# A two-layer encoder on one core: large tiles moved to multiples of 128 bytes, and a 64-row product given all 128 rows

## The chip, the core and the metric

The kernel runs on one core of a Trainium2 chip. The metric is the device time of one execution in microseconds (us), the median of several runs. Engines are named as in the profile: PE is TensorE (matmuls), PEld its weight loads, DVE is VectorE, ACT is ScalarE, SP issues most of the DMAs.

## What is computed

256 tokens of width 2048 go through two layers in float32. Each layer has a token mixer and a gated channel mixer with a short convolution:

```
x = x + rms_norm(mixer(rms_norm(x)))
x = x + rms_norm((gelu(conv3(h @ w_up_gate)) * (h @ w_up_val)) @ w_down)     h = rms_norm(x), d_ff 5632
```

The mixer of layer 0 has 8 heads of windowed attention and 8 query heads of grouped attention, head size 128. The mixer of layer 1 is latent attention with 16 heads. There a query and a key have 128 plain and 64 rotary dimensions, and the rotary key is shared by all heads:

```
q = concat(q_nope, rope(q_rope))        # 128 + 64
k = concat(k_nope, rope(k_rope))        # k_rope is the same for all heads
s = q @ k.T * 192 ** -0.5;  o = softmax(s) @ v
```

## The kernel before

**Products in parts.** Every float32 operand `a` of a matmul is split into a high part (a copy to float32r, on ACT) and a low part (`a` minus the high part, on DVE), and a product is made of three: high x high, high x low, low x high. `_split` (L117, L118) does this to each weight chunk of 128 x 1024, which SP loads into `raw`; the parts are `whi` and `wlo`, three buffers each. Four loops use them:
- `proj_tok` with `mm3` (L172 to L174): the stationary operand is a 128 x 128 piece of the activations (`xhl` before the mixers, `oh` and `ol` for the attention's output, `gh` and `gl` for the gated values), the moving one 512 columns of `whi` or `wlo`. It makes the input projections and all output projections.
- `proj_t` (L186, L187): stationary weights, moving activations. `xhl` holds high and low part side by side, so L186 streams 512 columns (both) against `whi` and L187 256 columns (high) against `wlo`. It makes the up-projections, 2816 pairs in the two layers.
- `proj_small` and `proj_pair` (L172 to L174 with 256 columns): the latent projections from `cq` and `ckv`.
- `attend` (L475 scores, L256 transposes, L172 to L174 with `pT` and `v`): one call for each of 32 heads, two half heads of 128 queries each.

**The rotary part of a score.** For a half head of layer 1 `scores` lists five products: three of the plain parts (`qk`), and two of the rotary parts. A rotary query in `qr` has its high part in rows 0 to 63 and its low part in rows 64 to 127. `kr[:, 0, :]` holds the high part of the key twice, in both halves of the rows; one 128-row matmul so makes high x high and low x high. `kr[:, 1, :]` holds the low part twice, and of it only rows 0 to 63 are wanted, with the query's high part: a 64-row matmul. `evac_kr` fills `kr` with one copy from PSUM (L819).

**Order.** Python generators hand out the attention's and the norms' steps between weight chunks (`tick`), and each engine runs its list in the order in which it was made. At the end of an output projection `out_proj` computes the norm's factor for each half of the tokens (`factor`, with its columns `posta`, `posts`, `postv`, `postu`), turns the new `x` by transposes, and fills waits of TensorE with matmuls on `zeros`.

**Where tiles lie.** Pools lie one behind the other in each partition of the on-chip memory, and a tile takes a multiple of 32 bytes. `const` holds `gains` (1664 bytes) and then `eps` and `spare` (32 bytes each); `act`, `wp` (weights) and `small` (columns, rows) follow, and the pools of a mixer or a ffn lie behind `small`. The table gives the first byte of each tile modulo 128, as built; all slices that a matmul takes begin at multiples of 128 bytes from it.

| tiles | before | after |
|---|---|---|
| `gains` | 0 | 0 |
| `zeros`, `ident`, `ident_r` | 64 | 0 |
| `xhl`, `m`, `qk`, `x`, `raw`, `whi`, `wlo` | 64 | 0 |
| in `small`: `junk`, `m3` | 0, 96 | 96, 64 |
| `gb` | 32 | 0 |
| all tiles of the mixers and ffns: `oh`, `ol`, `gh`, `gl`, `cq`, `ckv`, `kr`, `qr`, `q`, `k`, `kB`, `v`, `vB`, `p`, `pT`, `y`, tables | 96 | 0 |

Of the kernel before, what the change touches and what calls it, by code (L numbers as in the profile page):

```python
# [9 lines left out]
F32 = mybir.dt.float32  # L10
# [6 lines left out]
P = 128  # L17
# [20 lines left out]
class Model:  # L38
# [307 lines left out]
    def out_proj(self, nk, parts, post, pre, order=None, before={}):  # L346
# [6 lines left out]
        nc = self.nc  # L353
# [26 lines left out]
        r = []  # L380

        def factor(t):
            acc, s, v, u = (self.col(f"post{n}") for n in "asvu")
            r.append(self.col("postr"))
            self.square_sums(acc, ps[t])
            nc.scalar.activation(s, acc, AF.Sqrt, scale=1.0 / D, bias=part[:, t:t + 1])
            nc.vector.tensor_scalar(out=v, in0=acc, scalar1=1.0 / D, scalar2=part[:, t:t + 1],
                                    op0=ALU.mult, op1=ALU.add)
            nc.vector.scalar_tensor_tensor(out=u, in0=s, scalar=s, in1=v, op0=ALU.mult, op1=ALU.add)
            nc.vector.reciprocal(out=u, in_=u)  # L390
            return nc.vector.tensor_scalar(out=r[t], in0=s, scalar1=2.0, scalar2=u, op0=ALU.mult, op1=ALU.mult)
# [5 lines left out]

        full = slice(0, 512)
        factor(0)
        if pre is None:  # L400
            scaled(3, 0)
# [337 lines left out]
    def mixer1(self, pre):  # L739
        nc, tc, a = self.nc, self.tc, self.a  # L740
        with tc.tile_pool(name="mix1", bufs=1) as sp:
# [6 lines left out]
            cq = sp.tile([P, 4, 2, T], F32R, name="cq")  # L748
            ckv = sp.tile([P, 4, 2, T], F32R, name="ckv")
            kr = sp.tile([P, 2, T], F32R, name="kr")  # L750

            def latent(ps, row, out):
                g = sp.tile([P, 512], F32, tag="grow", name="grow", bufs=1)
                nc.sync.dma_start(out=g, in_=a["lat"][row:row + 1, :].broadcast_to([P, 512]))
                ss = self.small.tile([P, 2, 1], F32, tag="ls", name="ls", bufs=2)
                for t in range(2):
                    self.square_sums(ss[:, t, :], ps[t])
                rr = self.rstd_over(ss, self.r, 1, 512)
                whole = []
                for t in range(2):  # L760
                    y = sp.tile([P, 512], F32, tag="y", name="y", bufs=2)
                    nc.vector.scalar_tensor_tensor(out=y, in0=ps[t], scalar=rr[:, t, :], in1=g,
                                                   op0=ALU.mult, op1=ALU.mult)
                    whole.append(y)
                yield
                for k in range(0, 4, 2):
                    pt = self.psum("at").rearrange("p (i t) -> p i t", i=2)
                    for j in range(2):
                        for t in range(2):
                            self.turn_whole(pt[:, j, t * P:(t + 1) * P], whole[t][:, (k + j) * P:(k + j + 1) * P])  # L770
                    self.parted(out[:, k:k + 2, 0, :], out[:, k:k + 2, 1, :], pt)

            def rope(y, z, v, n):

                nc.vector.tensor_tensor(out=y, in0=v, in1=tab[:, :, 0].broadcast_to([P, 2, n, 64]), op=ALU.mult)
                for h in range(2):
                    d, f = slice(32 * h, 32 * h + 32), slice(32 - 32 * h, 64 - 32 * h)
                    nc.vector.tensor_tensor(out=z[:, :, :, d], in0=v[:, :, :, f],
                                            in1=tab[:, :, 1, :, d].broadcast_to([P, 2, n, 32]), op=ALU.mult)
                nc.vector.tensor_tensor(out=y, in0=y, in1=z, op=ALU.add)  # L780

            def room(tag, n):
                t = sp.tile([P, 512], F32, tag=tag, name=tag, bufs=2 if tag == "y" else 1)
                return t[:, :2 * n * 64].rearrange("p (t h f) -> p t h f", t=2, f=64)
# [12 lines left out]
            def evac_kr(ps):  # L797

                k, y, z = (room(tag, 1) for tag in ("grow", "y", "z"))
                raw = sp.tile([P, 512], F32, tag="p", name="raw", bufs=self.p_bufs)[:64]  # L800
                nc.scalar.copy(raw[:, T:], ps[:64, T:])
                nc.vector.tensor_tensor(out=raw[:, :T], in0=ps[:64, :T], in1=raw[:, T:], op=ALU.add)
                yield
                v = self.psum("at")[:, :2 * 64].rearrange("p (t f) -> p t f", t=2)
                for t in range(2):
                    nc.tensor.transpose(v[:, t, :], raw[:, t * P:(t + 1) * P], self.ident[:64, :64])
                hl = sp.tile([P, 2, 512], F32R, tag="hl", name="hl", bufs=2)
                tok = hl[:, 0, :].rearrange("p (t a b f) -> p t a b f", t=2, a=2, b=2)
                for t in range(2):
                    nc.scalar.activation(k[:, t, 0, :], v[:, t, :], AF.Copy, scale=self.r[:, t:t + 1])  # L810
                rope(y, z, k, 1)
                for b in range(2):
                    self.parted(tok[:, :, 0, b, :], tok[:, :, 1, b, :], y[:, :, 0, :])
                yield
                pt = self.psum("at", F32R).rearrange("p (a t) -> p a t", a=2)
                for b in range(2):
                    for t in range(2):
                        self.turn(pt[:, b, t * P:(t + 1) * P], tok[:, t, b].rearrange("p b f -> p (b f)"))
                nc.scalar.copy(kr, pt.bitcast(F32))  # L819

            def evac_qr(v, qr):
                v = v.rearrange("p t (h f) -> p t h f", f=64)
# [21 lines left out]
            for p in range(8):  # L844
                if p % 2 == 0:
                    qr = []
                    evqr = self.evac(evac_qr(self.proj_small(part(cq), 256, 4), qr), 1, heads[-8:-4])
                qk, v, v_gen = [], [], []

                def evac_qk(w, src, qk=qk, p=p):  # L850
                    if not qk:
                        qk.append(self.act.tile([P, 2, 2, 2, T], F32R, tag=f"xm{p % 4}", name="qk"))
                    self.parted(qk[0][:, src, :, 0, :], qk[0][:, src, :, 1, :], w)
                    yield

                def evac_v(w, v=v):
                    v.append(sp.tile([P, 2, 2, 256], F32R, tag="v", name="v", bufs=3))
                    self.parted(v[0][:, 0], v[0][:, 1], w)
                    yield

                eq = self.evac(evac_qk(self.proj_pair(part(cq)), 0), 1, heads[-8:-6])
                if p == 0:
                    self.finish(evkv)
                ek = self.evac(evac_qk(self.proj_pair(part(ckv)), 1), 1, (eq,))

                def head(h, qk=qk, v=v, qr=qr, v_gen=v_gen):
                    i = h % 2

                    def scores(b):
                        bs = slice(b * P, (b + 1) * P)  # L870
                        qt, kt = qk[0][:, 0, i], qk[0][:, 1, i]
                        return [(qt[:, 0, bs], kt[:, 0, :]), (qt[:, 0, bs], kt[:, 1, :]), (qt[:, 1, bs], kt[:, 0, :]),
                                (qr[0][:, h % 4, bs], kr[:, 0, :]), (qr[0][0:64, h % 4, bs], kr[0:64, 1, :])]

                    s = slice(i * P, (i + 1) * P)
                    yield from self.attend(scores, scale, None, lambda j: (v[0][:, 0, j, s], v[0][:, 1, j, s]),
                                           v_gen, o(h), sp)

                new = [self.later(head(h), (evkr, evqr, eq, ek)) for h in (2 * p, 2 * p + 1)]
                v_gen.append(self.evac(evac_v(self.proj_small(part(ckv), 256, 4)), 1, heads[-6:-4]))  # L880
                heads += new
# [38 lines left out]
    def run(self):  # L920
        nc, a = self.nc, self.a
        self.plan(self.all_chunks())
        self.x, self.xhl = [None] * 4, [None] * 4
        self.g = self.const.tile([P, G_ALL], F32, name="gains")
        nc.scalar.dma_start(out=self.g, in_=a["gains"])
        self.eps = self.const.tile([P, 1], F32, name="eps")
        nc.vector.memset(self.eps, EPS)
        self.spare = self.const.tile([P, 1], F32, name="spare")
        self.table(AF.Sqrt, self.eps)
        self.zeros = self.const.tile([P, T], BF16, name="zeros")  # L930
        nc.vector.memset(self.zeros, 0.0)
        self.warm(24)
        self.mixer0("l0_ffn_pre")
        self.ffn(0, "l1_mix_pre")
        self.mixer1("l1_ffn_pre")
        self.ffn(1, None)
        assert self.at == len(self.chunks)
# [81 lines left out]
```

## Time and profile before

| | |
|---|---|
| three runs | 2113.58, 2104.84, 2113.62 us; median 2113.58 |
| profiled execution | 2104.7 us, of which the span from first to last instruction 2102.9 |
| mean granted TensorE clock in it | 0.999 |
| busy: PE, DVE, ACT | 2090.2, 1342.3, 1081.8 us |
| HBM read | 381.96 MB, 183 GB/s over the span |

A busy TensorE is not a TensorE at its peak: the records of neighbouring matmuls overlap (a row of 394 ns begins 0.23 us ahead of the next), so the distance from one start to the next is the time that one takes. Rows of the order in time show start, duration, engine, line, operation, names (out, then moving and stationary operand, or the two of a tile alike), rows x columns of the stationary operand, and partitions x columns of the moving one.

### The profile page before, as it was taken

The page shows a single profiled execution, that of the slowest core. Times are in us where ns is not written, and L with a number is a line of the kernel's source. Part 1 is how long each engine was busy: PE and PEld are TensorE (multiplying, and loading weights), DVE is VectorE, ACT ScalarE, POOL GpSimd, SP SyncE. Part 2 cuts the span into 40 slices and gives each one's busy share as a digit, 9 for nine tenths or more (in the row PEclk, how much of TensorE's full clock was granted, in tenths as well). Part 3 has the DMA queues.
Part 4 walks back from the last instruction along what each step waited for, and adds up shares of the span by engine and source line. Part 5 has one row for each costly group of instructions (what it writes and reads, how often), then busy time and mean ns, then how long its engine had stood idle before and what let it go on. Part 6 is the DMA issues. An engine that isn't in the chain of part 4 may idle for free.

```text
span 2102.9 us, 29245 instructions
## 1 busy us (share of the span) xinstructions
PE 2090.2 (99%) x11121; PEld 1775.0 (84%) x11121; DVE 1342.3 (64%) x2050; ACT 1081.8 (51%) x1694; POOL 0.2 (0%) x4
## 2 busy tenths in 40 slices
PE   9999999999999999999999999999999999999998
PEld 7888888888888888888888998788888888888886
DVE  6876757667667676444476775676766667654444
ACT  7654546555555555334465554565555555544433
POOL 0000000000000000000000000000000000000000
PEclk9999999999999999999999999999999999999999
DMA  8545565666666666666665335566666666666664
GB/s 315 169 151 170 160 204 160 196 192 184 194 190 185 195 184 194 193 190 194 192 180 157 117 117 164 171 191 192 186 192 192 188 192 190 187 193 190 193 189 150
DMA packets 108718, 385.97 MB, mean 184 GB/s; under 512 B 12065, under 2 KB 12577, under 8 KB 108577
## 3 DMA queue, kind: packets, MB, share of 16 engines
q1 hardware_dynamic: 108288, 383.83, 60.4%
q8 instruction: 87, 1.43, 0.3%
q14 instruction: 55, 0.44, 0.1%
q10 hardware_dynamic: 288, 0.28, 0.0%
HBM read 381.96 MB, written 2.10 MB: 183 GB/s over the span
## 4 chain that ended last, share of the span: by engine, by line
PE 99%; DVE 1%; DMA 0%; ACT 0%; issue 0%; DVEq 0%; SPq 0%
PE ps L186 31%; PE ps L174 16%; PE ps L172 16%; PE ps L173 16%; PE ps L187 15%; PE ps L475 2%; PE ps L256 1%; DVE x L395 0%; PE ps L417 0%; DMA raw<-in_w_in 0%; PE ps L792 0%; PE ps L252 0%; ACT junk L296 0%; DVE xhl L529 0%; PE ps L793 0%
## 5 line engine op out<-in xcount | busy, mean ns | idle before, releaser
L118 DVE TENSOR_TENSOR wlo<-raw,whi 128x1024 fp32r<-128x1024 f32 (+1 forms) x710 | 867.3, 1222 | 702.0 <-ACT whi L117 700.5
L117 ACT CAST whi<-raw 128x1024 fp32r<-128x1024 f32 (+1 forms) x710 | 743.7, 1048 | 817.7 <-PE ps L174 439.4
L186 PE MATMUL ps<-xhl,whi 128*128 128x512 f32 x2816 | 978.6, 394 | 1.0 <-DVE xhl L529 1.0
L187 PE MATMUL ps<-xhl,wlo 128*128 128x256 f32 x2816 | 779.2, 277 | 0.0
L186 PEld LDWEIGHTS ps<-xhl,whi 128*128 128x128 f32 x2816 | 527.6, 188 | 123.3 <-DVE xhl L529 2.0
L187 PEld LDWEIGHTS ps<-xhl,wlo 128*128 128x128 f32 x2816 | 528.7, 188 | 1.1 <-DVE wlo L118 0.5
L174 PE MATMUL ps<-whi,gl 128*128 128x512 f32 x704 | 280.9, 399 | 0.0
L173 PE MATMUL ps<-wlo,gh 128*128 128x512 f32 x704 | 277.4, 394 | 0.0
L172 PE MATMUL ps<-whi,gh 128*128 128x512 f32 x704 | 276.0, 392 | 0.0
L173 PEld LDWEIGHTS ps<-wlo,gh 128*128 128x128 f32 x704 | 132.2, 188 | 34.2
L172 PEld LDWEIGHTS ps<-whi,gh 128*128 128x128 f32 x704 | 132.2, 188 | 31.6
L174 PEld LDWEIGHTS ps<-whi,gl 128*128 128x128 f32 x704 | 132.2, 188 | 30.4
L172 PE MATMUL ps<-whi,xhl 128*128 128x512 f32 x352 | 138.9, 396 | 1.0 <-ACT whi L117 1.0
L173 PE MATMUL ps<-wlo,xhl 128*128 128x512 f32 x352 | 137.4, 390 | 0.0
L174 PE MATMUL ps<-whi,xhl 128*128 128x512 f32 x352 | 137.4, 391 | 0.0
L172 PE MATMUL ps<-whi,oh 128*128 128x512 f32 x256 | 102.3, 400 | 0.0
L174 PE MATMUL ps<-whi,ol 128*128 128x512 f32 x256 | 100.8, 394 | 0.0
L173 PE MATMUL ps<-wlo,oh 128*128 128x512 f32 x256 | 100.5, 393 | 0.0
L261 ACT COPY half<-ps 128x256 f32<-128x256 f32 x176 | 65.0, 369 | 45.7 <-PE ps L186 36.0
L172 PEld LDWEIGHTS ps<-whi,xhl 128*128 128x128 f32 x352 | 66.0, 188 | 14.7 <-ACT whi L117 1.3
L174 PEld LDWEIGHTS ps<-whi,xhl 128*128 128x128 f32 x352 | 66.0, 188 | 14.1
L173 PEld LDWEIGHTS ps<-wlo,xhl 128*128 128x128 f32 x352 | 66.2, 188 | 13.5 <-DVE wlo L118 0.9
(183 smaller groups left out, 1642.7 us busy)
## 6 DMA issues: line engine op xcount, KB each, us to landing
raw<-in_w_up SPq DMA_DIRECT2D x352, 512.0 KB, 4.2
raw<-in_w_down SPq DMA_DIRECT2D x176, 512.0 KB, 3.7
raw<-in_w_in SPq DMA_DIRECT2D x88, 512.0 KB, 3.7
raw<-in_w_out SPq DMA_DIRECT2D x64, 512.0 KB, 3.7
gb<-in_post SPq DMA_DIRECT2D x16, 256.0 KB, 3.6
raw<-in_w_qn SPq DMA_DIRECT2D x8, 512.0 KB, 3.7
raw<-in_w_kn SPq DMA_DIRECT2D x8, 512.0 KB, 3.7
raw<-in_w_v SPq DMA_DIRECT2D x8, 512.0 KB, 3.7
```

The source lines that it names most:

```text
L117: self.nc.scalar.copy(hi[:, s], raw[:, s])
L118: self.nc.vector.tensor_tensor(out=lo[:, s], in0=raw[:, s], in1=hi[:, s].bitcast(F32), op=ALU.subtract)
L172: mm(ps, lh, rh, start=start, stop=False)
L173: mm(ps, lh, rl, start=False, stop=False)
L174: mm(ps, ll, rh, start=False, stop=stop)
L186: mm(out[i], hi[:, s], x(k), start=k == 0, stop=False)
L187: mm(out[i][:, :T], lo[:, s], x(k)[:, :T], start=False, stop=k == nk - 1)
L256: self.tc.keep_in_program_order(self.nc.tensor.transpose(out, x, self.ident))
L261: self.nc.scalar.copy(b, ps[:, T:])
L475: nc.tensor.matmul(ps[:, i, :], l, r, start=n == 0, stop=n == len(pairs) - 1))
```

## The change

It moves tiles and changes one product:
- `eps` and `spare` become two columns of one tile `one` in the pool `small`, and the four columns of `factor` become one tile `post` of four columns. `const` then holds 64 bytes less ahead of what follows, and `small` is a multiple of 128 bytes long; the table above gives what comes of it.
- The rotary high queries times low keys product takes all 128 rows. Rows 64 to 127 of `kr[:, 1, :]` are set to zero by a memset, and `evac_kr` copies to `kr` in two pieces that leave them alone.

```
         def factor(t):
-            acc, s, v, u = (self.col(f"post{n}") for n in "asvu")
+            cols = self.col("post", 4)
+            acc, s, v, u = (cols[:, n:n + 1] for n in range(4))
             r.append(self.col("postr"))
...
             kr = sp.tile([P, 2, T], F32R, name="kr")
+            nc.vector.memset(kr[64:, 1, :].bitcast(F32), 0.0)
...
-                nc.scalar.copy(kr, pt.bitcast(F32))
+                nc.scalar.copy(kr[:, 0, :], pt[:, 0, :].bitcast(F32))
+                nc.scalar.copy(kr[0:64, 1, :], pt[0:64, 1, :].bitcast(F32))
...
-                                (qr[0][:, h % 4, bs], kr[:, 0, :]), (qr[0][0:64, h % 4, bs], kr[0:64, 1, :])]
+                                (qr[0][:, h % 4, bs], kr[:, 0, :]), (qr[0][:, h % 4, bs], kr[:, 1, :])]
...
-        self.eps = self.const.tile([P, 1], F32, name="eps")
+
+        one = self.small.tile([P, 2], F32, name="one", bufs=1)
+        self.eps, self.spare = one[:, 0:1], one[:, 1:2]
         nc.vector.memset(self.eps, EPS)
-        self.spare = self.const.tile([P, 1], F32, name="spare")
         self.table(AF.Sqrt, self.eps)
```

TensorE's and SP's instructions stand in the same order as before. DVE and ACT have one more each. On DVE it stands at the end of the first ffn, between the two calls of `factor` (L388 to L392 are one call's four columns; L396 adds the half of the tokens to `x`). After the change:

```order
L396 SCALAR_TENSOR_TENSOR x_342<-m_9209,postr,x_342 128x512
L118 TENSOR_TENSOR wlo<-raw,whi 128x1024
L752 MEMSET kr 64x256
L388 TENSOR_SCALAR post<-post,part 128x1
L390 SCALAR_TENSOR_TENSOR post<-post 128x1
L391 RECIPROCAL post<-post 128x1
```

The memset is the row that is new there. On ACT the copy to `kr` stands in the latent mixer between the parts of `qk` and the next weights' high part. Before:

```order
L523 CAST hl<-y 128x2x64 x2
L523 CAST qk<-ps 128x2x256
L819 CAST kr<-ps 128x512
L117 CAST whi<-raw 128x1024
L523 CAST hl<-y 128x8x64
```

And after:

```order
L524 CAST hl<-y 128x2x64 x2
L524 CAST qk<-ps 128x2x256
L821 CAST kr<-ps 128x256
L822 CAST kr<-ps 64x256
L117 CAST whi<-raw 128x1024
L524 CAST hl<-y 128x8x64
```

One copy has become two; nothing else there moved.

## The prediction

> **What bounds the kernel now.** I read the page first: busy shares and the chain of waits. Then the table of who waited for whom, and last the order of time on TensorE, because what matters here is how far apart its matmuls start.
>
> ```profile
> PE 2090.2 (99%) x11121; PEld 1775.0 (84%) x11121; DVE 1342.3 (64%) x2050; ACT 1081.8 (51%) x1694; POOL 0.2 (0%) x4
> PE 99%; DVE 1%; DMA 0%; ACT 0%; issue 0%; DVEq 0%; SPq 0%
> PE ps L417 <- DVE x L395: 1.4, 3, 0.7
> DVE wlo L118 <- ACT whi L117: 700.5, 535, 2.4
> ACT whi L117 <- PE ps L174: 439.4, 270, 3.0
> L186 PE MATMUL ps<-xhl,whi 128*128 128x512 f32 x2816 | 978.6, 394 | 1.0 <-DVE xhl L529 1.0
> L187 PE MATMUL ps<-xhl,wlo 128*128 128x256 f32 x2816 | 779.2, 277 | 0.0
> L174 PE MATMUL ps<-whi,gl 128*128 128x512 f32 x704 | 280.9, 399 | 0.0
> L172 PE MATMUL ps<-whi,xhl 128*128 128x512 f32 x352 | 138.9, 396 | 1.0 <-ACT whi L117 1.0
> L172 PE MATMUL ps<-whi,oh 128*128 128x512 f32 x256 | 102.3, 400 | 0.0
> ```
>
> TensorE is 99% of the chain, and its longest total wait for anyone is 1.4 us. DVE waits for ACT and ACT waits for TensorE, so those two run behind it with room to spare. Whatever shortens the distance between two matmuls shortens the span one for one; whatever happens on DVE, ACT or a queue costs nothing until TensorE waits for it. In the groups the mean of one (394 ns) is no guide, since neighbours overlap: I use the distance of starts instead. A name such as `whi,gl` is moving operand, then stationary one. L172 to L174 are issued in equal numbers for each pair of operands, so the groups stand for 3 x 704, 3 x 352 and 3 x 256 matmuls.
>
> The distances, taken from the first and the last row of steady stretches on TensorE:
>
> ```profile
> 25.83 0.39 PE L172 MATMUL ps<-whi,xhl 128*128 128x512 f32 x1
> ...
> 33.99 0.39 PE L172 MATMUL ps<-whi,xhl 128*128 128x512 f32 x1
> ...
> 289.80 0.40 PE L172 MATMUL ps<-whi,oh 128*128 128x512 f32 x1
> ...
> 297.50 0.40 PE L172 MATMUL ps<-whi,oh 128*128 128x512 f32 x1
> ...
> 500.14 0.28 PE L187 MATMUL ps<-xhl,wlo 128*128 128x256 f32 x1
> ...
> 507.77 0.28 PE L187 MATMUL ps<-xhl,wlo 128*128 128x256 f32 x1
> ...
> 899.63 0.39 PE L172 MATMUL ps<-whi,gh 128*128 128x512 f32 x1
> ...
> 907.33 0.39 PE L172 MATMUL ps<-whi,gh 128*128 128x512 f32 x1
> ...
> 1072.26 1.25 PE L156 MATMUL ps<-zeros 128*128 128x256 bf16 x10
> 1073.35 0.60 PE L417 MATMUL ps<-ident,x 128*128 128x128 f32 x4
> ...
> 1151.82 0.29 PE L172 MATMUL ps<-whi,ckv 128*128 128x256 f32 x1
> ...
> 1154.35 0.28 PE L172 MATMUL ps<-whi,ckv 128*128 128x256 f32 x1
> ...
> 1247.09 0.28 PE L173 MATMUL ps<-ckv,whi 128*128 128x256 f32 x1
> ...
> 1249.55 0.28 PE L173 MATMUL ps<-ckv,whi 128*128 128x256 f32 x1
> 1249.67 0.28 PE L174 MATMUL ps<-ckv,wlo 128*128 128x256 f32 x1
> 1249.79 0.28 PE L172 MATMUL ps<-pT,v 128*128 128x256 f32 x1
> ...
> 1251.11 0.28 PE L174 MATMUL ps<-pT,v 128*128 128x256 f32 x1
> ```
>
> Beside each pair stands where its operands lie (bytes mod 128, from the table of the kernel's layout):
> - 512 columns, moving 64, stationary 64 (`whi,xhl`): 36 steps in 8.16 us, 226.7 ns each.
> - 512 columns, moving 64, stationary 96 (`whi,oh` and `whi,gh`): 33 steps in 7.70 us, 233.3 ns each, both times.
> - 256 columns, 64 and 96 (`whi,ckv`): 21 steps in 2.53 us, 120.5 ns; 96 and 96 (`pT,v`): 11 steps in 1.32 us, 120.0 ns; 96 and 64 (`ckv,whi`): 21 steps in 2.46 us, 117.1 ns.
> - up-projection, a 512 and a 256 together, all at 64: 22 pairs in 7.63 us, 346.8 ns.
> - floor: ten bf16 matmuls of 256 columns in 1.09 us, 109.0 ns; so at most 218.0 ns for 512 columns.
>
> So a stationary operand at 96 costs 6.7 ns more than one at 64 where 512 columns stream, and about 3 ns more where 256 do; the moving operand at 96 shows no cost (117.1 is the lowest of its kind). No row shows a float32r operand at 0.
>
> **The change, part by part.** *The 64-row product.* 32 matmuls take 64 rows of `qr` and `kr`:
>
> ```profile
> L475 PE MATMUL ps<-kr,qr 64*128 64x256 f32 x32 | 12.2, 382 | 0.0
> L475 PE MATMUL ps<-kr,qr 128*128 128x256 f32 x32 | 9.0, 282 | 0.0
> 1146.90 0.62 PE L475 MATMUL ps<-qk 128*128 128x256 f32 x3
> 1147.35 0.59 PE L475 MATMUL ps<-kr,qr 128*128 128x256 f32 x2
> 1147.87 0.62 PE L475 MATMUL ps<-qk 128*128 128x256 f32 x3
> ...
> 1148.85 0.63 PE L475 MATMUL ps<-qk 128*128 128x256 f32 x3
> ```
>
> From 1146.90 to 1148.85 run two half heads of five matmuls each, 0.975 us per half head. Five 256-column matmuls without the 64-row form take 5 x 120.0 = 600 ns (the `pT,v` rows), so the one 64-row matmul, with the change of form before and after it, costs 375 ns. With 128 rows all five have one form: 32 x 0.375 = 12.0 us, all of it TensorE's own time. The 100 ns between the two means (382 and 282) would give only 3.2 us; I take the larger, since the distances contain the neighbours' delay and the means do not.
>
> A rule that speaks against this part: the Trainium skill, TensorE: Matmul & The Clock Gate, section LDWEIGHTS (loading the stationary operand), says that a load's time follows the columns and not the contraction rows. By that rule alone 64 rows cost what 128 do, this part brings 0 and the sum below would be 12.0 us higher; the 0.975 us of the half head disagrees.
>
> What it adds: a memset on DVE ahead of the second `factor` of the first ffn, and a second copy on ACT.
>
> ```profile
> 1071.58 1.22 DVE L118 TENSOR_TENSOR wlo<-raw,whi 128x1024 fp32r<-128x1024 f32 x1
> 1072.75 0.21 DVE L387 TENSOR_SCALAR postv<-posta,part 128x1 f32<-128x1 f32 x1
> 1072.02 0.60 ACT L296 ACTIVATE junk<-ps 128x512 bf16<-128x512 f32 x1 [1.75 <-PE ps L174]
> 1140.40 0.59 ACT L819 CAST kr<-ps 128x512 fp32r<-128x512 f32 x1 [0.53 <-PE ps L252]
> ```
>
> The memset waits for the last matmul of the ffn, and the square sum on ACT (1072.02) waits for the same one. DVE's next instruction, at 1072.75, needs that square sum, so DVE has an instruction's room there: by the nearest row, 0.2 us (256 elements without an input), it may finish by then or come a tenth late. The split at 1071.58 ends at 1072.80, so in the worst case `factor` starts 0.2 us later and TensorE, which here spins on the ten filler matmuls, ends 0.2 us later. The copy of 0.59 us becomes two, so at most 0.6 us more of ACT; ACT stood idle 0.53 us before it, and the first heads' scores (1146.90, above) follow over 5 us later. I count 0 for both, 0.3 us at most. The four `post` columns in one tile and `one` for `eps` and `spare` add no wait: the built program waits for the same events.
>
> *The offsets.* Order and number of all other instructions stay. Stationary operands that go from 96 to 0 take, at least, the place of those at 64: (2112 + 768) x (233.3 - 226.7) = 19.2 us. The 256-column ones with a stationary at 96 are, from the code, 32 x 6 for `pT,v`, 96 scores in layer 0, 64 of `kr,qr`, 192 of `whi,ckv` and 96 of `whi,cq`: 640 x 2.9 = 1.9 us.
>
> Unknown is what 0 gives against 64. Lower end: nothing, since 64 and 0 may be the same to the reader. Upper end: all down to the floor: 2816 x (346.8 - 327.0) = 55.8; 1056 x (226.7 - 218.0) = 9.2; 2880 x (233.3 - 218.0) = 44.1; 640 x 11.0 = 7.0; the 480 with stationary 64, x 8.1 = 3.9: in all 120.0 in place of 21.1 us. A loss is bounded by the row at 96 (a rival, below). I take the lower end, because the row nearest to an operand at 0 is one at 64 with both operands alike, and one more set of rows says that part of the excess at 64 is not the address:
>
> ```profile
> 1106.35 0.39 PE L173 MATMUL ps<-wlo,xhl 128*128 128x512 f32 x1
> ...
> 1107.51 0.39 PE L172 MATMUL ps<-whi,xhl 128*128 128x512 f32 x1
> ...
> 1109.32 0.39 PE L174 MATMUL ps<-whi,xhl 128*128 128x512 f32 x1
> ```
>
> Just behind a group of transposes the same operands at 64 first run 5 steps in 1.16 us, 232 ns each, and then 8 in 1.81 us, 226 ns each. The distance there settles with how loads and streams fall against each other, and a shift of both by the same 64 bytes leaves that as it is.
>
> Sum: 12.0 + 19.2 + 1.9 = 33.1 us off the profiled execution's 2104.7 us (span 2102.9): 2071.6. Two of the three timed runs lie 8.9 us above that execution (2113.6; the median), one at it; I add half of this, 4.4, and say 2076.
>
> **The rivals.**
> 1. Offsets from 128-byte lines count in full, and 0 reaches the floor. For it: the excess over 218.0 falls with the offset, 15.3 at 96 and 8.7 at 64. Against it: the rows behind the transposes, where the excess changes and the offsets don't, and the moving operand, which at 96 costs no more than at 64. Price: 12.0 + 120.0 = 132.0 off, 1972.7. With a floor a little lower for 512 columns than twice that of 256, 1960.
> 2. Offsets do nothing; `gh` and `oh` cost 233.3 for another reason, such as their distance from `whi`. Then only the 64-row part is left: 2092.7. The same comes out of the Trainium skill, SBUF — State Buffer, section SBUF: two separate sides, which gives the memory lines of 16 bytes: every offset here, before and after, is a multiple of 16. The 6.7 ns between 64 and 96 disagree.
> 3. Slower: an operand at 0 costs what one at 96 does. The 512-column matmuls now at 64 rise to 233.3: (1056 + 2816) x 6.6 = 25.6 more, 12.0 less, the others unchanged: 2118.3. It decides from 5.8 ns on for each of the 3872 (12.0 + 10.5, half a per cent). For it: no row at 0. Against it: alike offsets (64 and 64) are the quickest 512-column rows.
> 4. The 64-row part brings nothing, because the delay belongs to five matmuls from five tiles and not to the form: 2083.6. Against it: `pT,v` and the scores of layer 0 show no such stretch.
>
> **How the numbers follow.** Chances: the forecast 0.55, rival 1 0.27, rival 2 0.10, rival 3 0.05, rival 4 0.03. The range has to take in rival 1, without which 0.27 would be left out, and reaches at the other end to rival 2 with the 8.9 us of the slower runs: 1960 to 2100. The forecast's own range is 2062 to 2086. Half a per cent, 10.5 us, is about what a measurement of this kernel tells from no change. Faster: 0.55 + 0.27 + 0.06 of rival 2 (12.0 us is near that bound) + 0.03 = 0.91; same 0.05; slower 0.04.
>
> **What would show it.** Right: `whi,gh` and `whi,oh` start 226.7 ns apart, the up-projection's pair stays at 347, a half head takes 0.60 us, and no 64-row form is left in the groups. Rival 1: the pair falls to some 327 and `whi,xhl` to 218 or less. Wrong altogether: `whi,gh` still at 233.3 (rival 2), `whi,xhl` above 227 (rival 3), or TensorE waiting over 1 us for DVE near the first ffn's end.

## The result, and the profile after

The changed kernel takes 2074.4 us, the median of four runs (2074.27 to 2074.60). The four runs of the kernel before beside it had a median of 2109.2 us (two at 2104.8, two at 2113.6), which gives a ratio of 0.9835 with an interval of 0.9806 to 0.9864. Runs of one kernel lie on levels 9 us apart, and the experiments below show which instructions make that step; so I compare the lowest levels: 2104.8 with 2074.4, 30.4 us, and the profiled spans, 2102.9 with 2072.8, 30.1 us. The forecast was 2076.

The page of the changed kernel, the lines that answer to those shown of before: busy time of TensorE and its weight loads, the share of the chain of waits, and the costliest groups (busy time, mean of one, idle time ahead).

```profile
PE 2060.3 (99%) x11121; PEld 1772.1 (85%) x11121; DVE 1341.7 (65%) x2051; ACT 1083.5 (52%) x1695; POOL 0.2 (0%) x4
PE 98%; DVE 1%; DMA 0%; issue 0%; ACT 0%; DVEq 0%; SPq 0%
L186 PE MATMUL ps<-xhl,whi 128*128 128x512 f32 x2816 | 978.6, 394 | 1.0 <-DVE xhl L530 1.0
L187 PE MATMUL ps<-xhl,wlo 128*128 128x256 f32 x2816 | 779.2, 277 | 0.0
L174 PE MATMUL ps<-whi,gl 128*128 128x512 f32 x704 | 273.9, 389 | 0.0
L172 PE MATMUL ps<-whi,xhl 128*128 128x512 f32 x352 | 138.9, 396 | 0.5 <-ACT whi L117 0.5
L172 PE MATMUL ps<-whi,oh 128*128 128x512 f32 x256 | 99.9, 390 | 0.0
```

TensorE does as many matmuls as before and is still the whole chain. Two groups moved, `whi,gl` (280.9 to 273.9) and `whi,oh` (102.3 to 99.9); the up-projection and `whi,xhl` read the same to the last digit. These are durations that overlap, so the size of the gain has to be read from starts. Four places in the order of time on TensorE: the down-projection, the up-projection, the half heads of the first latent scores, and a 256-column projection.

```profile
889.72 0.39 PE L172 MATMUL ps<-whi,gh 128*128 128x512 f32 x1
...
892.44 0.39 PE L172 MATMUL ps<-whi,gh 128*128 128x512 f32 x1
...
499.61 0.40 PE L186 MATMUL ps<-xhl,whi 128*128 128x512 f32 x1
...
506.20 0.39 PE L186 MATMUL ps<-xhl,whi 128*128 128x512 f32 x1
...
1137.88 0.52 PE L476 MATMUL ps<-qk 128*128 128x256 f32 x3
1138.24 0.40 PE L476 MATMUL ps<-kr,qr 128*128 128x256 f32 x2
1138.48 0.52 PE L476 MATMUL ps<-qk 128*128 128x256 f32 x3
...
1139.08 0.52 PE L476 MATMUL ps<-qk 128*128 128x256 f32 x3
...
1141.60 0.28 PE L172 MATMUL ps<-whi,ckv 128*128 128x256 f32 x1
...
1144.36 0.28 PE L174 MATMUL ps<-whi,ckv 128*128 128x256 f32 x1
```

`whi,gh`: 12 steps in 2.72 us, 226.7 ns (233.3 before). Up-projection: 19 pairs in 6.59 us, 346.8 ns (346.8). A half head of five matmuls: 0.60 us (0.975). `whi,ckv`: 23 steps in 2.76 us, 120.0 ns (120.5).

Adding up the distance from each matmul's start to the next one's start, over the whole trace, gives the account (my sums over all 11121 matmuls, us; the total is about 9.5 us short of the span: 1.1 us ahead of the first matmul and 8.4 us behind the start of the last):

```
group of matmuls                      before    after   change   forecast
weights x gh,gl,oh,ol  (512 columns)   672.0    653.1    -18.9      -19.2
weights x xhl          (512 columns)   243.7    243.6     -0.1        0
up-projection pairs    (512 and 256)   985.7    985.7      0          0
kr,qr and qk                            31.1     19.7    -11.4      -12.0
other 256-column matmuls               116.6    116.5     -0.1       -1.9
transposes and fillers                  44.4     44.9     +0.4        0 (0.3 at most)
sum                                                      -30.0      -33.1
```

### The profile page after: what moved, and what is told of

The parts are those of the page before. It is cut to its first block, busy times and chain, and to the rows that moved or that the text cites. A ratio compares the mean times of both kernels' runs of the same rounds, so it can differ in the third digit from the quotient of the medians.

```text
span 2072.8 us, 29247 instructions
## 1 busy us (share of the span) xinstructions
PE 2060.3 (99%) x11121; PEld 1772.1 (85%) x11121; DVE 1341.7 (65%) x2051; ACT 1083.5 (52%) x1695; POOL 0.2 (0%) x4
## 4 chain that ended last, share of the span: by engine, by line
PE 98%; DVE 1%; DMA 0%; issue 0%; ACT 0%; DVEq 0%; SPq 0%
PE ps L186 31%; PE ps L172 16%; PE ps L173 16%; PE ps L174 16%; PE ps L187 16%; PE ps L476 1%; PE ps L256 1%; DVE x L396 1%; PE ps L418 0%; DMA raw<-in_w_in 0%; PE ps L794 0%; DVE wlo L118 0%; PE ps L252 0%; ACT junk L296 0%; DVE xhl L530 0%
## 5 line engine op out<-in xcount | busy, mean ns | idle before, releaser
L172 PE MATMUL ps<-whi,gh 128*128 128x512 f32 x704 | 273.9, 389 | 0.0
L174 PE MATMUL ps<-whi,gl 128*128 128x512 f32 x704 | 273.9, 389 | 0.0
L173 PE MATMUL ps<-wlo,gh 128*128 128x512 f32 x704 | 273.9, 389 | 0.0
L172 PE MATMUL ps<-whi,oh 128*128 128x512 f32 x256 | 99.9, 390 | 0.0
```

The lines of the kernel that those rows point to most:

```text
L172: mm(ps, lh, rh, start=start, stop=False)
L173: mm(ps, lh, rl, start=False, stop=False)
L174: mm(ps, ll, rh, start=False, stop=stop)
```

## The experiments

Two theories ran through them. By theory L it is an operand's own offset from a memory line that costs time; by theory R it is the distance between the addresses of the moving and the stationary operand of one matmul, and where both lie together does not matter. The kernel before could not tell them apart: its 226.7 ns rows had both operands at 64, its 233.3 ns rows one at 64 and one at 96.

**e1, the 64-row part alone; e2 and e8, the offsets alone.** e1 is the kernel before with the memset, the two copies and the full-row product. e2 is the changed kernel with these three taken back; e8 is the same kernel run again, for a second profile.

```
e1, in the kernel before:
+            nc.vector.memset(kr[64:, 1, :].bitcast(F32), 0.0)
-                nc.scalar.copy(kr, pt.bitcast(F32))
+                nc.scalar.copy(kr[:, 0, :], pt[:, 0, :].bitcast(F32))
+                nc.scalar.copy(kr[0:64, 1, :], pt[0:64, 1, :].bitcast(F32))
-                ... (qr[0][0:64, h % 4, bs], kr[0:64, 1, :])]
+                ... (qr[0][:, h % 4, bs], kr[:, 1, :])]
```

> The kernel before with the 128-row product alone; all tiles stay at 64 and 96. Theory of the prediction (the 64-row form costs 375 ns per half head, nothing else): the profiled span falls by 11.4 to 12.0 us to some 2091, gh and oh stay at 233.3 ns. Rival (the part of the change that counts is the offsets, the rows bring the 3.2 us of the means): 2099. If the two parts help or hinder each other, this run and the next do not add up to the 30.1 us of the whole change.

> The changed kernel with the 64-row product put back; all large tiles at 0. Theory of the prediction: gh and oh at 226.7 ns, span 18.9 us less than before (some 2084), the half head of layer 1 still 0.975 us. Rival (the gain of gh and oh needs nothing but other work beside it, not the offsets): no gain, 2103.

> The kernel of the second run once more, for a profile of one of its longer executions (2095 us in three of four, 2086 in the other). If the 9 us are a steady state of the up-projection as in the run with all tiles at 96, one layer's 1390 pairs are at 353 ns and the other's at 347, with the same operands; if not, the 9 us stand elsewhere.

e1 took 2092.25 us (span 2090.4, ratio 0.9913, interval 0.9883 to 0.9942), 12.5 us of span off. e2 took 2086.39 us once and 2095.2 to 2095.4 three times (ratio 0.9917, 0.9885 to 0.9948); the profiled execution was the quick one, span 2084.6, 18.3 us off. e8 took 2095.32 us. The two parts add up: 12.5 + 18.3 = 30.8 against 30.1. From the groups of e1 and then of e2:

```profile
L475 PE MATMUL ps<-kr,qr 128*128 128x256 f32 x64 | 12.8, 281 | 0.0
L174 PE MATMUL ps<-whi,gl 128*128 128x512 f32 x704 | 280.9, 399 | 0.0
```

```profile
L174 PE MATMUL ps<-whi,gl 128*128 128x512 f32 x704 | 273.9, 389 | 0.0
```

In e1 `whi,gl` stands where it stood before, in e2 where it stands after. In e1 the distances of `kr,qr` and `qk` fell by 11.7 us, those of the other 256-column matmuls by 0.8, and no other group moved by more than 0.2. In e2 the distances of `gh`, `gl`, `oh` and `ol` fell by 18.8 us, and all others rose by 0.5.

**e3, all large tiles together at 96.** One pad of 24 elements behind the gains moves every large tile of the changed kernel by 96 bytes, so that all distances between operands stay what they were.

```
         nc.scalar.dma_start(out=self.g, in_=a["gains"])
+        self.const.tile([P, 24], F32, name="pad0")
```

> The changed kernel with 96 unused bytes ahead of all tiles: every large tile at 96, moving and stationary operands alike. Theory R (what counts is where the two operands of a matmul lie relative to each other): no change, 2074, all 512-column matmuls with xhl, gh, oh at 226.7 ns. Theory L (a stationary operand at 96 crosses one line more than one at 0 or 64): all 512-column matmuls 6.6 ns longer: 1056 + 2880 + 2816 of them, 44.6 us, 2119.

It took 2083.4 to 2083.5 us three times and 2092.4 once (ratio 0.9882, 0.985 to 0.9913). The order of time of e3 on TensorE, the down-projection first and then the up-projection of each layer:

```profile
889.64 0.39 PE L172 MATMUL ps<-whi,gh 128*128 128x512 f32 x1
...
893.04 0.39 PE L172 MATMUL ps<-whi,gh 128*128 128x512 f32 x1
...
499.89 0.39 PE L186 MATMUL ps<-xhl,whi 128*128 128x512 f32 x1
...
506.47 0.40 PE L186 MATMUL ps<-xhl,whi 128*128 128x512 f32 x1
...
1499.82 0.40 PE L186 MATMUL ps<-xhl,whi 128*128 128x512 f32 x1
...
1506.54 0.40 PE L186 MATMUL ps<-xhl,whi 128*128 128x512 f32 x1
```

With both operands at 96, `whi,gh` starts every 226.7 ns (15 steps in 3.40 us), just as at 0. Theory L falls, and theory R holds for this term. The 8.9 us that e3 took more than the changed kernel are elsewhere: 19 pairs of the up-projection take 6.58 us in layer 0 (346.3 ns) and 6.72 us in layer 1 (353.7 ns), with the same code and the same offsets. Over each layer's 1390 pairs the sums are 483.4 and 492.4 us.

**e4, e5, e6, the weights alone shifted.** A pad ahead of the weight buffers and one behind them put `raw`, `whi` and `wlo` at 64, 32 or 96 past a line. The pads also moved `gh`, `gl`, `oh` and `ol` to 128 past a multiple of 256, so that their distance is not the weights' shift alone: moving minus stationary address, modulo 256, is 192, 160 and 224 for them in e4, e5 and e6, it is 192, 224 and 160 for the pairs, and 64, 32 and 96 for weights x `xhl`.

```
+        self.wp.tile([P, s // 4], F32, name="pad0")                       # s = 64, 32, 96
+        self.small.tile([P, (128 - s) // 4], F32, name="pad1", bufs=1)
```

> The changed kernel with the weight tiles (raw, whi, wlo) at 64 and all others at 0: the operands of every weight matmul lie 64 apart, the stationary ones at 0 (xhl, gh, oh, latents) or at 64 (weights). Theory L: 64 is as good as 0, no change, 2074. Theory R with a period of 64 bytes: no change either. Theory R with a period of 128 bytes: the 512-column matmuls change; from the one row that is known, 32 apart costs 6.6 ns, so up to 6.6 ns for each of 6752, 44.6 us more, or if 64 apart is a better place than 0, up to 8.7 ns less for each.

> The changed kernel with the weight tiles at 32 and all others at 0. The moving weights of the projections lie 32 bytes above their stationary operands, the moving activations of the up-projections 32 below. Theory R (the place of the two operands relative to each other, period 128): the up-projections, 32 below like gh and oh before, take 6.7 ns more a pair in both layers, 18 us; for the projections (3936 matmuls, 32 above) no run has shown it yet: 0 if only 'below' costs, 2092; 26 us more if the distance counts and not its sign, 2118. Theory S (the steady state that a stretch falls into is chance, and offsets only shift the chance): gh and oh at 226.7 or 233.3 by chance, the two layers not alike.

> The changed kernel with the weight tiles at 96 and all others at 0, the mirror of the run before: projections with the moving operand 32 below the stationary one (as gh and oh before the change), up-projections 32 above. Theory R: gh, oh and also xhl of the input projections at 233.3 ns, 3936 x 6.6 = 26 us more; the up-projections at 347 if only 'below' costs (2100), at 353 if the distance counts (2118).

They took 2109.9 us (ten runs, ratio 1.0007, 0.9992 to 1.0022), 2118.35 (four, 1.0057, 1.0037 to 1.0078) and 2096.95 (seven, 0.9958, 0.9945 to 0.9971), each within 0.3 us from run to run. Down-projection and up-projection of e4, then of e5, then of e6:

```profile
889.76 0.39 PE L172 MATMUL ps<-whi,gh 128*128 128x512 f32 x1
...
892.56 0.39 PE L172 MATMUL ps<-whi,gh 128*128 128x512 f32 x1
...
499.84 0.40 PE L186 MATMUL ps<-xhl,whi 128*128 128x512 f32 x1
...
506.55 0.40 PE L186 MATMUL ps<-xhl,whi 128*128 128x512 f32 x1
```

```profile
889.61 0.39 PE L172 MATMUL ps<-whi,gh 128*128 128x512 f32 x1
...
893.12 0.40 PE L172 MATMUL ps<-whi,gh 128*128 128x512 f32 x1
```

```profile
499.91 0.39 PE L186 MATMUL ps<-xhl,whi 128*128 128x512 f32 x1
...
506.50 0.39 PE L186 MATMUL ps<-xhl,whi 128*128 128x512 f32 x1
...
890.13 0.40 PE L172 MATMUL ps<-whi,gh 128*128 128x512 f32 x1
...
892.93 0.40 PE L172 MATMUL ps<-whi,gh 128*128 128x512 f32 x1
```

`whi,gh` starts every 233.3 ns in e4 and e6 (12 steps in 2.80 us) and 234.0 in e5 (15 in 3.51). The pair of the up-projection takes 353.2 ns in e4 (19 in 6.71 us) but 346.8 in e6 (19 in 6.59). The sums of start distances over the whole trace account for each kernel against the changed one (span 2072.8 us):

```
            w x gh..ol   w x xhl   pairs    others    sum     span
after          653.1      243.6     985.7    181.0   2063.3   2072.8
e4 (64)        672.0      245.2    1003.7    178.0   2098.8   2108.3
e5 (32)        674.6      249.1    1003.7    179.7   2107.1   2116.5
e6 (96)        671.9      249.4     985.5    179.0   2085.7   2095.2
```

So the 35.5 us between e4 and the changed kernel are 18.9 of the projections' weights, 18.0 of the pairs and 1.6 of `xhl`, less 3.0 of others. Of the values expected, e5's 2118 came, and e6 lies nearest to its 2100. The sums of weights x `xhl` give 232.2, 235.9 and 236.2 ns a matmul at 64, 32 and 96, against 230.7 in the changed kernel: 64 costs little there. Some 256-column matmuls get shorter when their operands are apart: in e4 the groups `w,ckv` (`w` is `whi` or `wlo`) go from 120.8 to 116.0 ns and `cq,w` from 121.9 to 118.3. In e5 `cq,w` and `ckv,w`, 96 apart, stay as they were (122.1 and 121.4 ns).

**e7, the 64-row product twice.** In the kernel before, each half head adds its 64-row product a second time.

```
-                ... (qr[0][0:64, h % 4, bs], kr[0:64, 1, :])]
+                ... *[(qr[0][0:64, h % 4, bs], kr[0:64, 1, :])] * 2]
```

> The kernel before with the 64-row product issued twice, one behind the other (it is added twice, so the scores differ in their low part). If the 375 ns of a half head are the price of going from 128 to 64 rows and back, the second 64-row matmul costs about one more matmul, 120 ns: 32 x 0.12 = 3.8 us more. If each 64-row matmul costs them, 32 x 0.375 = 12 us more.

It took 2108.9 us in its one run (span 2107.1, 4.2 more than before). The group of the 64-row form and two half heads of e7:

```profile
L475 PE MATMUL ps<-kr,qr 64*128 64x256 f32 x64 | 16.0, 330 | 0.0
```

```profile
1147.23 0.62 PE L475 MATMUL ps<-qk 128*128 128x256 f32 x3
1147.69 0.71 PE L475 MATMUL ps<-kr,qr 128*128 128x256 f32 x3
...
1149.43 0.62 PE L475 MATMUL ps<-qk 128*128 128x256 f32 x3
```

Two half heads take 2.20 us, 1.10 each, against 0.975 with one 64-row matmul. A second one right behind the first costs 0.12 us, as much as a 256-column matmul with all rows (120.0 ns). The 0.375 us are therefore the way into the form and out of it, not the form.

**e9, e10, the weights at 16 and at 112.** `whi` and `wlo` become slices of tiles that are 32 elements longer. Since 4224 bytes is 128 past a multiple of 256, the buffers alternate between 16 and 144 (e9) and between 112 and 240 (e10).

```
-        hi = self.wp.tile([P, 1024], F32R, ...)
+        hi = self.wp.tile([P, 1056], F32R, ...)[:, o:o + 1024]     # o = 4 (e9), 28 (e10); lo alike
```

> The changed kernel with whi and wlo at 16 and all others at 0: projections 16 bytes above, up-projections 16 below. Theory R with steps of 32 bytes: 16 falls with 0 or with 32, so 2074 or about 2118 (as with the weights at 32). Theory R in which the distance counts by degrees: between the two, some 2096.

> The changed kernel with whi and wlo at 112 and all others at 0: projections 16 bytes below, up-projections 16 above. With steps of 32 bytes 2074 or 2097 (as with the weights at 96); by degrees between. If a place beside 0 is better than 0, gh and oh under 226.7 ns or the pair under 346.7.

They took 2094.2 us (eight runs, ratio 0.9931, 0.9906 to 0.9957) and 2096.2 (eight, 0.9944, 0.9919 to 0.9969). The projections' sums are 663.0 and 660.9 us against 653.1, so 230.3 and 229.6 ns a matmul: between the 226.8 of distance 0 and the 233.4 of 96, 192 and 224. The pairs' sums, 994.5 and 998.4 us, lie between those of the changed kernel (985.7) and of e4 (1003.7).

**e11, the changed kernel again.**

> The changed kernel once more, in five rounds, for the two steady states of the up-projection. If both operands at 0 exclude the longer one, all runs lie at 2074. If it is chance there as with all tiles at 96 and with the offsets alone, about four in ten runs lie 9 us higher, at 2083.

Six runs: 2083.40 and five from 2074.36 to 2074.75 (ratio 0.9835, 0.9801 to 0.987). The profile is of the 2083.40. Layer 0 and then layer 1 of its up-projection:

```profile
499.69 0.40 PE L186 MATMUL ps<-xhl,whi 128*128 128x512 f32 x1
...
506.41 0.40 PE L186 MATMUL ps<-xhl,whi 128*128 128x512 f32 x1
...
1499.89 0.39 PE L186 MATMUL ps<-xhl,whi 128*128 128x512 f32 x1
...
1506.47 0.40 PE L186 MATMUL ps<-xhl,whi 128*128 128x512 f32 x1
```

19 pairs in 6.72 us (353.7 ns) in layer 0 and in 6.58 (346.3) in layer 1. The first profile of the same kernel had 346.8 in layer 0. The sums, 492.4 and 483.4 us against 483.4 and 483.4, explain the 8.8 us between the spans (2081.6 and 2072.8). One run in six lay higher, where four in ten had been expected if it were chance; six runs don't tell the two rates apart. e8 against e2 shows the same in layer 1: 492.4 against 483.4, with spans of 2093.5 and 2084.6.

**e12, the distances that looked best, together.** From the rows so far: distance 0 for the 512-column projections, a distance other than 0 for the 256-column matmuls, and for the pairs a distance of 32, which e6's 160 would be if 128 bytes were a period. The `xhl` of the ffn and `cq` and `ckv` become slices of longer tiles.

```
+            o = 8 if "ffn" in pre else 0
+            whole = self.act.tile([P, 2080], F32R, tag=f"xm{c}", ...)
+            self.xhl[c] = whole[:, o:o + 2048].rearrange(...)
...
-            cq = sp.tile([P, 4, 2, T], F32R, name="cq")
+            cq = sp.tile([P, 2080], F32R, name="cq")[:, 16:2064].rearrange(...)     # ckv alike
```

> The changed kernel with xhl at 32 in the two ffns alone (the moving operand of the up-projections 32 bytes above the weights, as in the run with the weights at 96, whose runs were all alike) and the latents cq and ckv at 64 (64 apart from the weights). Theory R: the up-projections stay at 347 ns a pair and lose the longer state, so all runs lie within 0.5 us; the 672 latent matmuls take 116 to 118 in place of 120 to 121 ns, 2.9 us less: 2071.5. Rival (the longer state is excluded by where the weights lie and not by the distance): 2071.5 with some runs at 2080.

It took 2075.1 us (2075.04 to 2075.20 in four runs; ratio 0.9852, 0.9828 to 0.9876), no quicker than the changed kernel. Input projections of the first layer and `whi,ckv` of e12:

```profile
24.63 0.39 PE L172 MATMUL ps<-whi,xhl 128*128 128x512 f32 x1
...
28.57 0.40 PE L174 MATMUL ps<-whi,xhl 128*128 128x512 f32 x1
...
30.43 0.39 PE L173 MATMUL ps<-wlo,xhl 128*128 128x512 f32 x1
...
33.61 0.39 PE L172 MATMUL ps<-whi,xhl 128*128 128x512 f32 x1
...
1144.24 0.28 PE L172 MATMUL ps<-whi,ckv 128*128 128x256 f32 x1
...
1146.16 0.28 PE L174 MATMUL ps<-whi,ckv 128*128 128x256 f32 x1
```

`whi,ckv` came down to 112.9 ns (17 steps in 1.92 us), over the whole trace `w,ckv` to 114.9 ns from 120.8; all matmuls but the 512-column projections and the pairs are 3.4 us less in sum. But a tile of 8320 bytes puts every second `xhl` 128 bytes past a multiple of 256. The first 17 steps above, at distance 128, take 231.8 ns each, the later 14, at distance 0, take 227.1. Over the whole trace, each matmul of weights x `xhl` beside the same one of the changed kernel, the 528 at a distance of 128 went from 227.8 to 232.9 ns on average, the 264 at 256 from 235.1 to 235.2 and the 264 at 0 from 232.1 to 232.8 (the last two means contain some longer steps). So 256 counts as 0, and 128 does not. That cost 2.9 us, and the pairs cost 0.9 more. All four runs of e12 lie on one level; since nine in ten of the changed kernel do too, that doesn't show that the longer level is gone.

## Why the prediction was right

*What bounds it.* TensorE carried the chain before and after, and 30.0 of the span's 30.1 us are distances between its matmuls.

*The 512-column term (19.2 forecast, 18.9 measured).* Right in size. The forecast took the row with both operands alike as the price of 0, and that is what came, in every group. Its wording, "a stationary operand at 96 costs 6.7 ns more than one at 64", was wrong in the cause: e3 puts all operands at 96 and pays nothing in this group. The 6.7 ns belong to the two operands lying 96 bytes apart, modulo 256. It is rival 2's doubt ("their distance from `whi`") that named the cause; its outcome failed since the change removes that distance too. The reason given for the lower end was that a common shift leaves the distances as they are, and e3 shows this for this group; that it is because of how loads and streams fall against each other isn't shown.

*The 64-row term (12.0 and 11.4).* Right, and so was the choice of 375 ns over the 100 ns between the means. The changed kernel's half head takes the 0.60 us that were named. e7 adds that the price is that of the change of form. The Trainium skill's page TensorEngine Tiling (Array Packing), section Key Properties, says that a switch of tiling mode needs a drain; the 0.375 us for two changes of form around one 64-row matmul agree with it. By the rule that the prediction took from the Trainium skill's page TensorE: Matmul & The Clock Gate, section LDWEIGHTS (loading the stationary operand), this part would have brought nothing. That rule is one on a load's time alone, and e1's 12.5 us disagree with taking it for the time of the whole matmul.

*The 256-column term (1.9 and 0.1).* Mis-sized: the step "about 3 ns more where 256 do" rested on one stretch of `ckv,whi` at 117.1 ns. Over the whole trace of before the mean of `ckv,w` is 121.6 ns, and 121.4 after. These two hide parts of opposite sign: the 64-row part alone brings the mean to 119.2 (e1), the offsets alone to 123.4 (e2). For `ckv,w` distance 0 is so even the dearer place (121.4 after against 119.2 in e1, and 116.8 in e12), and the offsets had no gain to bring.

*The additions counted at nothing.* The two copies did fit:

```profile
1131.64 0.38 ACT L821 CAST kr<-ps 128x256 fp32r<-128x256 f32 x1 [0.51 <-PE ps L252]
1131.91 0.37 ACT L822 CAST kr<-ps 64x256 fp32r<-64x256 f32 x1
```

0.64 us in place of 0.59, with ACT idle ahead of them. The memset did not. DVE at the end of the first ffn, in the changed kernel; then the transposes on TensorE that wait for it there, and the same ones in the kernel before:

```profile
1062.30 1.22 DVE L118 TENSOR_TENSOR wlo<-raw,whi 128x1024 fp32r<-128x1024 f32 x1
1063.63 0.27 DVE L752 MEMSET kr<- 64x256 f32 x1
1063.94 0.21 DVE L388 TENSOR_SCALAR post<-post,part 128x1 f32<-128x1 f32 x1
```

```profile
1065.50 0.44 PE L418 MATMUL ps<-ident,x 128*128 128x128 f32 x2 [0.92 <-DVE x L396]
```

```profile
1074.32 0.44 PE L417 MATMUL ps<-ident,x 128*128 128x128 f32 x2 [0.36 <-DVE x L395]
```

Before, the small multiply of `factor` followed the split at once (1071.58 to 1072.75, 1.17 us); now it comes 1.64 us after the split's start, since the memset stands between. TensorE waits 0.92 us there in place of 0.36. That it is the memset is shown by the others: e1, which has it, waits 0.82 us, and e2 and e8, which don't, 0.42. The forecast allowed 0.2 us, or 0.3 in all; this place costs 0.56, and 0.4 are left when the other boundaries, a little shorter, are taken in.

*The 4.4 us added for longer runs.* This did not come: the changed kernel ran at 2074.3 to 2074.8 in nine of ten runs. The 2071.6 of the sum missed the profiled 2074.6 by 3.0 us (roughly: the 256-column term 1.8, the 64-row term 0.6, the boundaries 0.4, the 512-column term 0.3), and the 4.4 made that up by chance. Taken by its steps the forecast was 3 us too hopeful.

*The rivals.* Rival 1 (0 reaches the floor) fails: pairs at 346.8, `whi,xhl` unchanged. Rival 3 (0 costs what 96 does) fails by the same rows, rival 4 by e1. By the 16-byte lines of the Trainium skill, SBUF — State Buffer, section SBUF: two separate sides, e4, e5 and e6 would have taken the changed kernel's time, as their shifts are multiples of 16; they took 2097 to 2118 us.

## What to carry to other kernels

Where TensorE is the bound, measure from start to start: here durations of 389 and 399 ns hid steps of 226.7 and 233.3. For such streams look at the difference of the two operands' addresses (here modulo 256 bytes), not at each one's alignment; "multiples of 128" did well here because the tiles that meet (`xhl`, `whi`, `gh`) fell on multiples of 256, and a longer buffer that alternates by 128 loses part of it again. Put one odd-shaped matmul among full ones only if it saves more than its two changes of form, and place a small write that nobody waits for where the engine is idle, not ahead of a chain that TensorE waits on.

## What the runs showed of the hardware that was not expected

*The distance of the operands.* Start distance of 512-column projections by (moving address - stationary address) mod 256, in the same kernel family:

```
distance   where                         ns
0          after, e3: w x gh..ol         226.8 (mean of 2879)
96         before, e1: w x gh..ol        233.4
160        e5                            234.3
192        e4                            233.4
224        e6                            233.4
16, 144    e9, in turn                   228.9 and 232.0 (230.3 together)
112, 240   e10, in turn                  229.2 and 230.0 (229.6 together)
128        e12: half of w x xhl          232.9 (mean of 528; 227.8 at 0)
64         e4: w x xhl                   232.2 (mean of 1056; 230.7 at 0)
32         e5: w x xhl                   235.9 (the same)
96         e6: w x xhl                   236.2 (the same)
```

The means of weights x `xhl` contain some longer steps, so they are to be read against their own value at 0. No simple rule fits all of them, and why 0 itself, at 226.7 ns in steady stretches, stays 8.7 ns above twice the bf16 matmul's 109.0 wasn't found. Open is also which stationary operand counts. TensorE's weight loads are busy 1772.1 of the 2072.8 us, so a load mostly runs while another matmul streams; in these streams a matmul's own stationary operand and the next one's lie alike, and the runs don't tell the two apart.

*Two cadences of one stream.* The up-projection's pair of matmuls runs at 347 or at some 353.6 ns, and a layer keeps the one it has for all its 490 us: 483.4 or 492.4 us. At distance 0 either was seen in one and the same program: the changed kernel and e11, e2 and e8, and the two layers of e3. At a distance of 192 (e4) and of 224 (e5) both layers of the profiled run have the longer one and all fourteen runs fit it; at 160 (e6) all seven fit the shorter. The levels of the kernel before (in the set with most runs 17 of 23 at 2104.6 to 2105.2 us, four at 2113.6 to 2113.8, two at 2122.5) are some 8.9 us apart, which is what none, one or both layers in the longer cadence would give; e8, e11 and e3 show it in the trace, but no execution of the kernel before on a higher level was profiled. What decides a layer's cadence at distance 0 stays open.
